# Two plain up tiles ahead of the block sums, and convolution taps in alternation, in a hybrid encoder step

## The chip, the cores and the metric

The kernel runs on one core of a Trainium2 chip. The metric is the device time of one execution in microseconds (us). TensorE multiplies matrices, VectorE (DVE), ScalarE (ACT) and GpSimd (POOL) do elementwise work, SyncE (SP) issues the transfers.

## The reference

One step of an encoder layer for 1024 prompt and 64 sample frames (1088 in all) of width 1024, everything in float32. Four mixers, then attention over a memory of 256 tokens, then a feed-forward part:

```
p = rmsnorm(x) @ w_in                       # split over conv, forgetting attention, HGRN2, stick-breaking
x = x + concat(conv, fox, hgrn, sb) @ w_out
x = x + mem_attend(rmsnorm(x), mk, mv)      # ... @ w_mo at its end
x = x + square(relu(rmsnorm(x) @ w_up)) @ w_down      # 1024 -> 4096 -> 1024
y = rmsnorm(x)
```

The convolution mixer is depthwise over 256 channels with 31 taps: each output frame is the sum of 31 inputs times a weight per channel, plus a bias; a layer norm and silu follow.

## The kernel before

Activations stand with the channels on the 128 partitions and the frames along the row. The frames are cut into group 0 (512 frames) and group 1 (576). Float32 products are made from rounded halves: `split` writes a high part (a cast on ScalarE, L74) and a low part (a subtraction on VectorE, L171), and each block product is three matmuls: high times high, high times low, low times high.

The program is written in Tile: a planner at build time orders each engine's instructions. Among those that are ready it takes the one with the smallest priority number; the number grows with every instruction written, and `tc.cur_priority += n` puts what follows n steps behind. Buffers are slots of a pool per tag ("ap" 16, "xt" 16, "aq" 12, "tm" 4 slots of 576 columns); an instruction waits until its slot is free. Weight tiles have two raw slots (`wr`) and two slots each for the halves (`wh`, `wl`).

**The mixers** (to about 670 us) run as four interleaved lanes: projections, attention, convolution (`lane_conv`) and HGRN2. A lane yields an estimated duration and the lane that is behind goes on; `yield Need(slot)` waits for a projection. The convolution has three blocks of frames (352, 352, 414 columns) and two channel halves (`ct`). Each half is an accumulation in one tile `y`: one instruction for the first tap (L770), 30 for the others (L773), each reading the `y` that the one before wrote. The two halves are written one after the other, and the layer norm (L788 on) needs both.

**The seam.** `dense_add(1, w_mo, ..., after=forms)` (L1297) adds the second half of the memory output product to group 1 for eight weight tiles m in the order 0, 4, 1, 5, 2, 6, 3, 7, stores the row (L1101) and calls `forms(m)` 600 priority steps back. For every m this adds the row's square to a running sum (L1049 to L1054); for m of 4 and above it norms rows k and k + 4 of group 1 (L1075) and builds the operand sums of the next product (L1286 to L1295).

**The up products.** The 32 up tiles go in pairs. With two halves of the width and the two frame groups, a pair is a 2 x 2 by 2 x 2 block product, made from seven instead of eight block products (i, the pair, runs from 0 to 15). The operand sums are T1 to T4; B11, B21 are group 0's halves (`h3`) and B22 the lower half of group 1; the weights have sums S1 to S4 (`sums`, `wform`). Two of the seven products need only group 0 (L1341, L1346 or L1357: bank `W`); the others are made by `mul2` in two strips of 288 columns. Pairs 0 and 1 have an order of their own (`i < 2`). Pair 0 also forms the norm factor `q` of group 1 (L1361 to L1364); it is applied to the results (L1321). The hidden rows go to DRAM (L1379).

Of the kernel before, what the change touches and what calls it, by code (L numbers as in the profile page):

```python
# [17 lines left out]
P = 128  # L18
# [9 lines left out]
CW = 31  # L28
# [24 lines left out]
def kernel(ctx: ExitStack, tc: tile.TileContext, *args):  # L53
# [688 lines left out]
    def lane_conv():  # L742
        tails = [None, None]
        for t0, np_ in ((0, 352), (352, 352), (704, 320)):
            last = t0 + np_ == SP
            n, nt = (CE, np_ + SS) if last else (np_, np_)
            ys, exts = [], []
            for ct in range(2):
                yield Need(ct)
                yield Need(2 + ct)  # L750
                ext = ct_(f"ext{ct}", f"ce{ct}", CE + HW)
                if t0 == 0:
                    V.memset(ext[:, :HW], 0.0)
                else:
                    V.tensor_copy(out=ext[:, :HW], in_=tails[ct])
                nc.sync.dma_start(out=ext[:, HW:HW + np_], in_=pj_d[ct][:, t0:t0 + np_])
                if last:
                    V.tensor_copy(out=ext[:, HW + np_:CE - SS + HW], in_=hT[:, ct])
                    nc.sync.dma_start(out=ext[:, CE - SS + HW:], in_=pj_d[ct][:, SP:T])
                gg, sg = ct_("gg", f"cy{ct}"), ct_("sg", "c0")  # L760
                nc.sync.dma_start(out=gg[:, :nt], in_=pj_d[2 + ct][:, t0:t0 + nt])
                sigmoid(sg[:, :nt], gg[:, :nt])
                V.tensor_tensor(out=ext[:, HW:HW + np_], in0=ext[:, HW:HW + np_], in1=sg[:, :np_], op=ALU.mult)
                if last:
                    V.tensor_tensor(out=ext[:, CE - SS + HW:], in0=ext[:, CE - SS + HW:], in1=sg[:, np_:nt], op=ALU.mult)
                else:
                    tails[ct] = hc.tile([P, HW], F32, name=f"tl{ct}", tag=f"tl{ct}", bufs=2)
                    V.tensor_copy(out=tails[ct], in_=ext[:, n:n + HW])
                y = ct_(f"y{ct}", f"cy{ct}")
                V.tensor_scalar(out=y[:, :n], in0=ext[:, 0:n], scalar1=cwT[:, ct, 0:1], scalar2=cvec[:, 0, ct:ct + 1],  # L770
                                op0=ALU.mult, op1=ALU.add)
                for j in range(1, CW):
                    V.scalar_tensor_tensor(out=y[:, :n], in0=ext[:, j:j + n], scalar=cwT[:, ct, j:j + 1], in1=y[:, :n],  # L773
                                           op0=ALU.mult, op1=ALU.add)
                    if j % 3 == 2:
                        yield 0.15 + n / 300.0
                ys.append(y[:, :n])
                exts.append(ext)
            if last:
                for at, dst in ((np_, conv_p), (CE, conv_s)):  # L780
                    ps = ps_cv.tile([P, G], F32, name="pco", tag="cv")
                    for ct in range(2):
                        nc.tensor.transpose(ps[:HW, ct * P:(ct + 1) * P], exts[ct][:, at:at + HW], ident)
                    ot = ct_("cvo", "c0")
                    V.tensor_copy(out=ot[:HW, :G], in_=ps[:HW])
                    nc.sync.dma_start(out=dst[0, 0], in_=ot[:HW, :G])
            rs = ct_("rs", "c0").rearrange("p (j n) -> p j n", j=2)
            sqs = [ct_(f"sq{ct}", f"ce{ct}", CE + HW) for ct in range(2)]  # L788
            for p0, pn in ((0, n // 2), (n // 2, n - n // 2)):
                yp = [y[:, p0:p0 + pn] for y in ys]  # L790
                sq = [s[:, p0:p0 + pn] for s in sqs]
                pm = ps_cv.tile([P, 512], F32, name="pme", tag="cv")
                for ct in range(2):
                    mm(pm[:, :pn], ones, yp[ct], ct == 0, ct == 1)
                for ct in range(2):
                    V.scalar_tensor_tensor(out=yp[ct], in0=pm[:, :pn], scalar=-1.0 / G, in1=yp[ct],
                                           op0=ALU.mult, op1=ALU.add)
                    act(sq[ct], yp[ct], AF.Square)
                pv2 = ps_cv.tile([P, 512], F32, name="pva", tag="cv")
                for ct in range(2):  # L800
                    mm(pv2[:, :pn], ones, sq[ct], ct == 0, ct == 1)
                v, r, t = rs[:, 0], sq[0], rs[:, 1]
                rstd_chain(None, pn, pv2[:, :pn], "xxx", scale=1.0 / G, out=r, tiles=(v, t))
                for ct in range(2):
                    V.tensor_tensor(out=yp[ct], in0=yp[ct], in1=r, op=ALU.mult)
                    V.tensor_scalar(out=yp[ct], in0=yp[ct], scalar1=cvec[:, 1, ct:ct + 1],
                                    scalar2=cvec[:, 2, ct:ct + 1], op0=ALU.mult, op1=ALU.add)
                for ct in range(2):
                    sigmoid(sq[ct], yp[ct])
                    V.tensor_tensor(out=yp[ct], in0=yp[ct], in1=sq[ct], op=ALU.mult)  # L810
                    if not last or p0 == 0:
                        nc.sync.dma_start(out=mix_d[ct][:, t0 + p0:t0 + p0 + pn], in_=yp[ct])
                    else:
                        nc.sync.dma_start(out=mix_d[ct][:, t0 + p0:SP], in_=ys[ct][:, p0:np_])
                        nc.sync.dma_start(out=mix_d[ct][:, SP:T], in_=ys[ct][:, CE - SS:])
                    yield 0.5 + pn / 150.0
# [449 lines left out]
    hb = {B11: h3[:4], B21: h3[4:]}  # L1266
    for f in (T2, T1, B22):
        hb[f] = [[late.pop(0)() for _ in range(2)] for k in range(4)]
    for f in (T3, T4):
        hb[f] = [[unit("xt" if k else "ap", F32R) for _ in range(2)] for k in range(4)]  # L1270

    sums2 = []

    def forms(m):

        if m == 0:
            sums2.append(add_square(1, 0, None, unit("tm")))
        else:
            add_square(1, m, sums2[0], unit("tm"))
        if m < 4:  # L1280
            return
        k = m - 4
        (h11, h12), (h21, h22) = ((xw[0][i], xw[1][i]) for i in (k, k + 4))
        for i in (k, k + 4):
            normed(1, i, g_ffn, rm1, 0, N2, xw[1][i])
        V.tensor_tensor(out=h11[:, :N1], in0=h12[:, :N1], in1=h11[:, :N1], op=ALU.subtract)  # L1286
        act(h11[:, N1:], h12[:, N1:], AF.Copy)
        split(*hb[T1][k], h11)
        V.tensor_tensor(out=h12, in0=h22, in1=h12, op=ALU.subtract)
        split(*hb[B22][k], h22)  # L1290
        V.tensor_tensor(out=h22, in0=h22, in1=h11, op=ALU.subtract)
        split(*hb[T2][k], h22)
        split(*hb[T3][k], h12)
        V.tensor_tensor(out=h21[:, :N1], in0=h21[:, :N1], in1=h22[:, :N1], op=ALU.subtract)
        split(hb[T4][k][0][:, :N1], hb[T4][k][1][:, :N1], h21[:, :N1])  # L1295

    dense_add(1, w_mo, HALF * P, KD - HALF, om[HALF:], ps1, store=True, after=forms)  # L1297
    pm1.close()
    psm = ctx.enter_context(tc.tile_pool(name="psm", bufs=2, space=PSUM))
    tc.cur_priority += 1200  # L1300
    for t in t1s:
        Q.memset(t[:, N1:], 0.0)

# [20 lines left out]
    def plus(out, a, b, eng=V):  # L1324
        eng.tensor_tensor(out=out, in0=a, in1=b, op=ALU.add)  # L1325

    for i in range(NU):
        r1 = fetch_w(w_up, 0, KD, 2 * i * P)
        r2 = fetch_w(w_up, 0, KD, (2 * i + 1) * P)
        pa, pb = ([wp.tile([P, KD, P], F32R, name=nm, tag=nm) for nm in ("wh", "wl")] for _ in range(2))  # L1330
        split(*pa, r1)
        s1 = fz.tile([P, 4, P], F32, name="s1", tag="s1", bufs=1)
        sums(r1[:, :4], r1[:, 4:], r2[:, :4], r2[:, 4:], s1, V)
        S2, S1 = wform(r1[:, :4]), wform(s1)
# [6 lines left out]
        mul(W, [t[:, :4] for t in pa], hb[B11], True, slice(0, N1))  # L1341
        act(t1[:, :N1], W, AF.Copy)
        c12, c22 = unit("ap"), unit("ap")
        if i < 2:

            mul(W, [t[:, 4:] for t in pa], hb[B21], False, slice(0, N1))  # L1346
            Y = banks()
            mul2(Y, S4, hb[B22], True)
            plus(halves(c12), halves(t1), Y[:, :, :HN])
        mul2(Z, S2, hb[T2], True)  # L1350
        plus(halves(c12), halves(c12 if i < 2 else t1), Z[:, :, :HN])
        mul2(X, S1, hb[T1], True)
        plus(halves(c22), halves(t1), X[:, :, :HN])
        if i < 2:
            plus(halves(c12), halves(c12), X[:, :, :HN])
        else:
            mul(W, [t[:, 4:] for t in pa], hb[B21], False, slice(0, N1))  # L1357
        c11 = unit("xt")
        square(c11[:, :N1], W)
        if i == 0:  # L1360
            q = rms_stats(1, psm, "w", s2=sums2[0])  # L1361
            rms = unit("tm")
            nc.sync.dma_start(out=rms, in_=rms_d)
            V.tensor_tensor(out=q, in0=q, in1=rms, op=ALU.mult)  # L1364
        mul2(Z, S3, hb[T3], False)
        plus(halves(c22), halves(c22), Z[:, :, :HN])
        square(c22, c22, q)
        if i >= 2:
            mul2(X, S4, hb[B22], False)
            plus(halves(c12), halves(c12), X[:, :, :HN])  # L1370
        square(c12, c12, q)
# [2 lines left out]
        plus(c21[:, :HN], t1[:, :HN], Z[:, 0, :HN])  # L1374
        plus(c21[:, HN:N1], t1[:, HN:N1], Z[:, 1, :N1 - HN])
        square(c21[:, :N1], c21[:, :N1])
        for m, g, t in ((0, 0, c11), (0, 1, c12), (1, 0, c21), (1, 1, c22)):
            t0, n, _ = GR[g]
            nc.sync.dma_start(out=hid_d[2 * i + m][:, t0:t0 + n], in_=t[:, :n])  # L1379
    fz_ctx.close()  # L1380


# [122 lines left out]
```

## Time and profile before

| | |
|---|---|
| median of 3 runs | 1795.35 us (1791.69 to 1795.78) |
| profiled execution, its own time | 1796.39 us |
| its span, first to last instruction | 1794.7 us |
| TensorE matmuls busy | 1721.9 us (96%) |
| VectorE busy | 1179.9 us (66%) |
| ScalarE busy | 793.2 us (44%) |
| GpSimd busy | 103.2 us (6%) |
| mean granted TensorE clock | 0.987 |

The span lies within the profiled execution's time; 1.7 us are outside it. Matmuls overlap in the pipeline, so their durations add up to more than their spacing; what one costs is read from the distance of their starts.

### The profile page before, as it was taken

What the parts mean: (1) busy time and instruction counts of PE and PEld (TensorE: products, weight loads), DVE (VectorE), ACT (ScalarE), POOL (GpSimd) and SP (SyncE); (2) the same over time, 40 slices, a digit from 0 to 9 for tenths busy, and PEclk for the clock granted to TensorE, in tenths of its full rate; (3) what the DMA queues carried; (4) which work ended last, traced back from release to release, by engine and by line L of the source; (5) the groups of instructions that cost most, each with busy time, mean ns of one, the idle gap of its engine ahead of it and who ended that gap; (6) DMA issues with size and microseconds to landing.
All of it is one profiled execution on the core that took longest, in us unless ns stands there. A gap on an engine that the chain in (4) does not pass through costs nothing.

```text
span 1794.7 us, 29493 instructions
## 1 busy us (share of the span) xinstructions
PE 1721.9 (96%) x11463; PEld 1511.7 (84%) x11475; DVE 1179.9 (66%) x2242; ACT 793.2 (44%) x1615; POOL 103.2 (6%) x201
## 2 busy tenths in 40 slices
PE   7999999999999999999999959999999999999997
PEld 5877757887877788988899949999999999999987
DVE  6455779888979886667777796555556544444435
ACT  6464566456356764346456343433344221222213
POOL 3011202000320210000000000000000000000000
PEclk9999999999999999999999989999999999999999
DMA  8221212222232448232522413333234823332112
GB/s 251 78 78 37 65 47 76 70 68 80 64 116 89 141 139 279 87 95 65 159 77 72 123 49 106 104 116 106 98 97 168 294 90 97 98 97 67 42 35 100
DMA packets 227307, 184.86 MB, mean 103 GB/s; under 512 B 16478, under 2 KB 196127, under 8 KB 227167
## 3 DMA queue, kind: packets, MB, share of 16 engines
q1 hardware_dynamic: 226911, 182.96, 32.7%
q8 instruction: 90, 1.47, 0.3%
q14 instruction: 50, 0.41, 0.1%
q0 software_dynamic: 256, 0.01, 0.0%
HBM read 132.45 MB, written 50.44 MB: 102 GB/s over the span
## 4 chain that ended last, share of the span: by engine, by line
PE 57%; DVE 5%; DMA 2%; ACT 1%; issue 1%; POOL 0%; SPq 0%; DVEq 0%; ACTq 0%; POOLq 0%
PE pz L71 23%; PE pw L71 16%; PE pa L71 8%; PE pq L71 5%; PE pmo L71 1%; PE pms L71 1%; DMA kr<-mkT_d 1%; PE pm L71 1%; DVE wl L171 1%; DVE ap L171 0%; PE pmt L1160 0%; PE pz L1430 0%; DVE tm L1075 0%; ACT wh L74 0%; DMA mix_d<-ho 0%
## 5 line engine op out<-in xcount | busy, mean ns | idle before, releaser
L74 ACT ACTIVATE wh<-wr 128x1024 fp32r<-128x1024 f32 (+1 forms) x180 | 161.4, 905 | 436.5 <-PE pz L71 196.3
L171 DVE TENSOR_TENSOR wl<-wr,wh 128x1024 fp32r<-128x1024 f32 (+1 forms) x180 | 184.6, 1032 | 70.8 <-ACT wh L74 69.8
L71 PE MATMUL pw<-ap,wh 128*128 128x512 f32 x704 | 219.7, 393 | 1.3 <-ACT t L74 0.7
L71 PE MATMUL pz<-ap,wh 128*128 128x288 f32 x960 | 192.5, 294 | 0.4 <-DVE ap L1325 0.4
L71 PE MATMUL pa<-ap,wh 128*128 128x256 f32 (+2 forms) x768 | 187.6, 332 | 2.6 <-DVE xt L1099 2.2
L71 PE MATMUL pm<-hx,wh 128*128 128x512 f32 (+1 forms) x640 | 176.3, 363 | 1.1 <-DVE hx L283 0.8
L71 PE MATMUL pm<-ap,wh 128*128 128x256 f32 (+1 forms) x768 | 164.2, 307 | 0.6 <-ACT vn L74 0.6
L71 PEld LDWEIGHTS pz<-ap,wh 128*128 128x128 f32 x960 | 156.7, 188 | 5.3 <-DVE ap L1325 0.8
L71 PEld LDWEIGHTS pw<-ap,wh 128*128 128x128 f32 x704 | 127.8, 189 | 23.7 <-ACT t L74 1.1
L71 PEld LDWEIGHTS pa<-ap,wh 128*128 128x128 f32 x768 | 132.9, 192 | 13.5 <-DVE xt L1099 2.4
L71 PE MATMUL pw<-ap,wl 128*128 128x512 f32 x352 | 138.1, 392 | 5.6 <-DVE wl L171 5.6
L71 PE MATMUL pz<-ap,wl 128*128 128x288 f32 x480 | 141.0, 294 | 0.0
L71 PEld LDWEIGHTS pm<-ap,wh 128*128 128x128 f32 x768 | 123.5, 191 | 5.4 <-issue 2.1
L71 PE MATMUL pa<-ap,wl 128*128 128x512 f32 (+2 forms) x384 | 127.2, 332 | 0.0
L71 PEld LDWEIGHTS pm<-hx,wh 128*128 128x128 f32 x640 | 110.2, 191 | 19.7 <-issue 1.9
L1325 DVE TENSOR_TENSOR xt<-xt,pz 128x576 f32<-128x576 f32 x56 | 42.2, 753 | 115.5 <-PE pz L71 111.0
L71 PE MATMUL pm<-ap,wl 128*128 128x256 f32 (+1 forms) x384 | 114.1, 297 | 0.0
L71 PE MATMUL pm<-hx,wl 128*128 128x512 f32 (+1 forms) x320 | 112.3, 351 | 0.0
L773 DVE SCALAR_TENSOR_TENSOR y<-ext,cwT,y 128x352 f32<-128x352 f32 (+1 forms) x180 | 106.4, 607 | 1.6
L1325 DVE TENSOR_TENSOR xt<-xt,pw 128x512 f32<-128x512 f32 (+2 forms) x80 | 51.0, 638 | 69.8 <-PE pw L71 67.7
L71 PE MATMUL pq<-ap,wh 128*128 128x512 f32 (+2 forms) x384 | 93.0, 331 | 0.0
L74 ACT ACTIVATE sba<-sba 128x127 f32<-128x127 f32 (+8 forms) x102 | 68.1, 682 | 52.8 <-DVE sba L490 52.0
(376 smaller groups left out, 3645.1 us busy)
## 6 DMA issues: line engine op xcount, KB each, us to landing
wr<-in_w_up_dram SPq DMA_DIRECT2D x32, 512.0 KB
wr<-in_w_down_dram SPq DMA_DIRECT2D x32, 512.0 KB
wr<-in_w_in_dram SPq DMA_DIRECT2D x24, 512.0 KB
hid_d<-ap SPq DMA_DIRECT2D x32, 288.0 KB
aq<-hid_d SPq DMA_DIRECT2D x32, 288.0 KB
wr<-in_w_out_dram SPq DMA_DIRECT2D x16, 512.0 KB
wr<-in_w_mq_dram SPq DMA_DIRECT2D x16, 512.0 KB
wr<-in_w_mo_dram SPq DMA_DIRECT2D x32, 256.0 KB
```

The source lines that it names most:

```text
L71: nc.tensor.matmul(out, lhsT=lhsT, rhs=rhs, start=start, stop=stop, **kw)
L74: nc.scalar.activation(out=out, in_=in_, func=func, **kw)
L171: V.tensor_tensor(out=lo, in0=src, in1=hi.bitcast(F32), op=ALU.subtract)
L773: V.scalar_tensor_tensor(out=y[:, :n], in0=ext[:, j:j + n], scalar=cwT[:, ct, j:j + 1], in1=y[:, :n], op0=ALU.mult, op1=ALU.add)
L1325: eng.tensor_tensor(out=out, in0=a, in1=b, op=ALU.add)
```

## The change

Pair 0 is no longer made from block sums. Its two tiles are plain products over the whole width: for group 0 with `h3`, for group 1 with the normed rows themselves. For that, all eight rows of group 1 are normed and split (four into the new pairs `b12`, four into B22 as before), in `second(m)` right after each row is complete. The operand sums (`forms`, now without norm and B22) are written in pair 1, after its first weight split, and 800 priority steps back; the step of 1200 ahead of the pairs is gone. Pair 1 keeps the order that pairs 0 and 1 had. In the convolution the taps of the two channel halves alternate, so both halves' projections have to be there before the first tap. The slots for T3 and T4 are taken after the output product.

```diff
                     V.tensor_copy(out=tails[ct], in_=ext[:, n:n + HW])
-                y = ct_(f"y{ct}", f"cy{ct}")
-                V.tensor_scalar(out=y[:, :n], in0=ext[:, 0:n], ...)
-                for j in range(1, CW):
-                    V.scalar_tensor_tensor(out=y[:, :n], in0=ext[:, j:j + n], scalar=cwT[:, ct, j:j + 1], in1=y[:, :n],
-                                           op0=ALU.mult, op1=ALU.add)
-                    if j % 3 == 2:
-                        yield 0.15 + n / 300.0
-                ys.append(y[:, :n])
+                ys.append(ct_(f"y{ct}", f"cy{ct}")[:, :n])
                 exts.append(ext)
+            for j in range(CW):
+                for ct, (y, ext) in enumerate(zip(ys, exts)):
+                    if j == 0:
+                        V.tensor_scalar(out=y, in0=ext[:, 0:n], ...)
+                    else:
+                        V.scalar_tensor_tensor(out=y, in0=ext[:, j:j + n], scalar=cwT[:, ct, j:j + 1], in1=y,
+                                               op0=ALU.mult, op1=ALU.add)
+                if j % 3 == 2:
+                    yield 0.3 + n / 150.0
...
-    for f in (T3, T4):
-        hb[f] = [[unit("xt" if k else "ap", F32R) for _ in range(2)] for k in range(4)]
+    b12 = [pair(1) for k in range(4)]
     sums2 = []
-    def forms(m):
+    def second(m):
         if m == 0:
             sums2.append(add_square(1, 0, None, unit("tm")))
         else:
             add_square(1, m, sums2[0], unit("tm"))
-        if m < 4:
-            return
-        k = m - 4
+        normed(1, m, g_ffn, rm1, 0, N2, xw[1][m])
+        split(*(hb[B22][m - 4] if m >= 4 else b12[m]), xw[1][m])
+    def forms(k):
         (h11, h12), (h21, h22) = ((xw[0][i], xw[1][i]) for i in (k, k + 4))
-        for i in (k, k + 4):
-            normed(1, i, g_ffn, rm1, 0, N2, xw[1][i])
...
-        split(*hb[B22][k], h22)
...
-    dense_add(1, w_mo, HALF * P, KD - HALF, om[HALF:], ps1, store=True, after=forms)
+    dense_add(1, w_mo, HALF * P, KD - HALF, om[HALF:], ps1, store=True, after=second)
     pm1.close()
     psm = ctx.enter_context(tc.tile_pool(name="psm", bufs=2, space=PSUM))
-    tc.cur_priority += 1200
+    for f in (T3, T4):
+        hb[f] = [[unit("xt" if k else "ap", F32R) for _ in range(2)] for k in range(4)]
...
-    for i in range(NU):
+    def store_hidden(i, tiles):
+        for m, g, t in zip((0, 0, 1, 1), (0, 1, 0, 1), tiles):
+            t0, n, _ = GR[g]
+            nc.sync.dma_start(out=hid_d[2 * i + m][:, t0:t0 + n], in_=t[:, :n])
+    ws = [load_w(w_up, 0, KD, m * P) for m in range(2)]
+    tiles = [unit("ap") for _ in range(4)]
+    for m in range(2):
+        W = bank()
+        mul(W, ws[m], hb[B11] + hb[B21], True, slice(0, N1))
+        square(tiles[2 * m][:, :N1], W)
+    q, rms = rms_stats(1, psm, "w", s2=sums2[0]), unit("tm")
+    nc.sync.dma_start(out=rms, in_=rms_d)
+    V.tensor_tensor(out=q, in0=q, in1=rms, op=ALU.mult)
+    for m in range(2):
+        Z = banks()
+        mul2(Z, ws[m], b12 + hb[B22], True)
+        square(halves(tiles[2 * m + 1]), Z[:, :, :HN], halves(q))
+    store_hidden(0, tiles)
+    for i in range(1, NU):
         r1 = fetch_w(w_up, 0, KD, 2 * i * P)
         r2 = fetch_w(w_up, 0, KD, (2 * i + 1) * P)
         pa, pb = ([wp.tile([P, KD, P], F32R, name=nm, tag=nm) for nm in ("wh", "wl")] for _ in range(2))
         split(*pa, r1)
+        if i == 1:
+            tc.cur_priority += 800
+            for k in range(4):
+                forms(k)
```

Further down `i < 2` becomes `i == 1`, the statistic of pair 0 (L1360 to L1364) leaves the loop, and the loop's stores go through `store_hidden`.

## Rows read from the trace of the kernel before

**Rows 1.** The page's strip: TensorE's busy tenths in 40 slices of 44.9 us.

```profile
PE   7999999999999999999999959999999999999997
```

**Rows 2.** Windows over the seam: busy us of each engine, granted clock, share and rate of DMA.

```profile
1040.00:1050.00 10.00, 1.44 (x2) 0.50 (x2) 10.00 (x16) 4.44 (x8) 0.00 (x0) 0.50 0.00 0
...
1033.40:1080.00 46.60, 27.65 (x156) 23.29 (x157) 43.65 (x69) 20.93 (x37) 0.00 (x0) 0.82 0.17 51
```

**Rows 3.** TensorE's waits, 1033 to 1080 us: in total, times, longest.

```profile
PE pr L71 <- DVE tm L1054: 10.7, 1, 10.7
PE pw L71 <- DVE wl L171: 5.6, 1, 5.6
...
PE pw L71 <- ACT t L74: 0.7, 1, 0.7
```

**Rows 4.** TensorE's timeline in the seam: start, us, what, idle before and releaser.

```profile
1033.92 0.70 PE L71 MATMUL pw<-ap,wh 128*128 128x512 f32 x2 [0.61 <-ACT wh L74]
1045.29 1.44 PE L71 MATMUL pr<-tm,ones 128*128 128x320 f32 x2 [10.67 <-DVE tm L1054]
...
1052.96 1.05 PE L71 MATMUL pw<-ap,wh 128*128 128x512 f32 x2
...
1055.52 0.71 PE L71 MATMUL pw<-ap,wh 128*128 128x512 f32 x2
...
1058.64 0.61 PE L71 MATMUL pw<-ap,wh 128*128 128x512 f32 x2
...
1059.32 0.61 PE L71 MATMUL pw<-ap,wh 128*128 128x512 f32 x2
...
1060.91 0.70 PE L71 MATMUL pr<-tm,ones 128*128 128x256 f32 x2 [0.75 <-ACT xt L74]
1061.94 0.53 PE L71 MATMUL pz<-fz,wh 128*128 128x288 f32 x2 [0.34 <-ACT wh L74]
...
1063.36 0.42 PE L71 MATMUL pz<-fz,wh 128*128 128x288 f32 x2
...
1064.94 0.43 PE L71 MATMUL pz<-fz,wh 128*128 128x288 f32 x2
```

**Rows 5.** VectorE's timeline: first and last of its run, two spacings.

```profile
1013.67 0.82 DVE L1075 SCALAR_TENSOR_TENSOR xt<-xt,g_ffn,tm 128x576 f32<-128x576 f32 x1 [0.46 <-DMA x_d<-xt]
...
1035.20 0.75 DVE L171 TENSOR_TENSOR fz<-xt,fz 128x576 fp32r<-128x576 f32 x1
1035.87 0.75 DVE L171 TENSOR_TENSOR xt<-xt 128x576 fp32r<-128x576 f32 x1
...
1051.09 1.22 DVE L171 TENSOR_TENSOR wl<-wr,wh 128x1024 fp32r<-128x1024 f32 x1
1052.22 0.75 DVE L171 TENSOR_TENSOR fz<-xt,fz 128x576 fp32r<-128x576 f32 x1
...
1062.66 0.68 DVE L171 TENSOR_TENSOR ap<-wr,ap 128x512 fp32r<-128x512 f32 x1
```

**Rows 6.** The statistic's operations on tile tm: min/median/max ns.

```profile
L152 DVE TENSOR_TENSOR tm<-tm x2: 424/458/493, 1063.8 to 1065.6; 128x320 f32<-128x320 f32 x1, 128x256 f32<-128x256 f32 x1
```

**Rows 7.** The chain that ended last, one transfer of it: start, us.

```profile
1063.37 4.59 DMA wr<-in_w_up_dram
```

**Rows 8.** SP's timeline behind the seam.

```profile
1076.30 2.86 SPq L1379 DMA_DIRECT2D hid_d<-ap  x2
```

**Rows 9.** VectorE's timeline in the mixers: runs of taps.

```profile
323.97 4.92 DVE L773 SCALAR_TENSOR_TENSOR y<-ext,cwT,y 128x352 f32<-128x352 f32 x8
...
454.81 2.56 DVE L773 SCALAR_TENSOR_TENSOR y<-ext,cwT,y 128x352 f32<-128x352 f32 x5
```

**Rows 10.** Windows: L773 alone (VectorE, clock, DMA); then all engines.

```profile
300.00:345.00 45.00, 14.29 (x25) 0.92 0.22 67
...
520.00:540.00 20.00, 16.41 (x138) 13.75 (x138) 17.64 (x38) 10.22 (x29) 10.16 (x12) 1.00 0.27 86
```

**Rows 11.** SP's timeline: the loads of group 1's mixer outputs.

```profile
677.16 5.16 SPq L1016 DMA_DIRECT2D aq<-mix_d  x8
```

More of the change, by code (lines that the diff above doesn't have):

```diff
@@ L768, in lane_conv @@
                     V.tensor_copy(out=tails[ct], in_=ext[:, n:n + HW])
-                y = ct_(f"y{ct}", f"cy{ct}")
-                V.tensor_scalar(out=y[:, :n], in0=ext[:, 0:n], scalar1=cwT[:, ct, 0:1], scalar2=cvec[:, 0, ct:ct + 1],
-                                op0=ALU.mult, op1=ALU.add)
-                for j in range(1, CW):
-                    V.scalar_tensor_tensor(out=y[:, :n], in0=ext[:, j:j + n], scalar=cwT[:, ct, j:j + 1], in1=y[:, :n],
-                                           op0=ALU.mult, op1=ALU.add)
-                    if j % 3 == 2:
-                        yield 0.15 + n / 300.0
-                ys.append(y[:, :n])
-                exts.append(ext)
+                ys.append(ct_(f"y{ct}", f"cy{ct}")[:, :n])
+                exts.append(ext)
+            for j in range(CW):
+                for ct, (y, ext) in enumerate(zip(ys, exts)):
+                    if j == 0:
+                        V.tensor_scalar(out=y, in0=ext[:, 0:n], scalar1=cwT[:, ct, 0:1], scalar2=cvec[:, 0, ct:ct + 1],
+                                        op0=ALU.mult, op1=ALU.add)
+                    else:
+                        V.scalar_tensor_tensor(out=y, in0=ext[:, j:j + n], scalar=cwT[:, ct, j:j + 1], in1=y,
+                                               op0=ALU.mult, op1=ALU.add)
+                if j % 3 == 2:
+                    yield 0.3 + n / 150.0
             if last:
@@ L1343 @@
         c12, c22 = unit("ap"), unit("ap")
-        if i < 2:
+        if i == 1:
             mul(W, [t[:, 4:] for t in pa], hb[B21], False, slice(0, N1))
@@ L1350 @@
         mul2(Z, S2, hb[T2], True)
-        plus(halves(c12), halves(c12 if i < 2 else t1), Z[:, :, :HN])
+        plus(halves(c12), halves(c12 if i == 1 else t1), Z[:, :, :HN])
         mul2(X, S1, hb[T1], True)
         plus(halves(c22), halves(t1), X[:, :, :HN])
-        if i < 2:
+        if i == 1:
             plus(halves(c12), halves(c12), X[:, :, :HN])
@@ L1359 @@
         square(c11[:, :N1], W)
[L1360 to L1364, printed above, removed]
         mul2(Z, S3, hb[T3], False)
@@ L1367 @@
         square(c22, c22, q)
-        if i >= 2:
+        if i > 1:
             mul2(X, S4, hb[B22], False)
@@ L1376 @@
         square(c21[:, :N1], c21[:, :N1])
-        for m, g, t in ((0, 0, c11), (0, 1, c12), (1, 0, c21), (1, 1, c22)):
-            t0, n, _ = GR[g]
-            nc.sync.dma_start(out=hid_d[2 * i + m][:, t0:t0 + n], in_=t[:, :n])
+        store_hidden(i, (c11, c12, c21, c22))
     fz_ctx.close()
```

## The prediction, made before the change was run

> **What bounds the kernel now.** I read the page's strip of slices first. TensorE is at 9 tenths nearly everywhere; the one deep hole after the start is slice 24, about 1032 to 1077 us [rows 1]. A table by windows sizes it: from 1033.4 to 1080 TensorE is busy 27.65 of 46.60 us, so 18.95 us are idle, and from 1040 to 1050 the granted clock is 0.50, the 1.2 GHz level [rows 2]. That is the seam between the second memory output product (dense_add, L1297) and the first pair of up tiles. The waits name the cause: 10.7 us for a sum of squares (L1054) and 5.6 us for a weight split (L171), both on VectorE, and 0.7 us for a ScalarE copy [rows 3]. The timeline of VectorE shows why: its queue runs without a hole worth naming from 1013.67 to about 1063.3, through the operand sums (`forms`) that all seven products of the first pair need [rows 5]. So in this seam VectorE's queue is the bound; before and behind it, TensorE.
>
> The timeline of TensorE also gives the prices [rows 4]. At full clock three 512-column matmuls take 1059.32 − 1058.64 = 0.68 us, 0.227 each; twelve of 288 columns take 1064.94 − 1063.36 = 1.58, 0.132 each (those of 224 I price by columns, 0.102). At the lower level six of 512 take 1055.52 − 1052.96 = 2.56, 0.427 each. About ten ran so: 10 × 0.20 = 2.0 us. The statistic's first product lost another 0.6 (1.44 us, against 0.70 × 320/256 = 0.88 at the later one's rate). The seam thus loses 18.95 + 2.0 + 0.6 = 21.55 us. That is the pool from which the change can draw.
>
> **The change, part by part.**
>
> *TensorE's own work.* A pair by block sums is 24 products of 512 columns (5.44 us), 96 of 288 (12.64), and 12 each of 288 and 224 (2.81): 20.89 us. The plain pair is 48 of 512 (10.88) and 96 of 288 (12.64): 23.52 us. The change adds 2.63 us for good; only i = 0 is exchanged, and i = 1 keeps the early form that both i < 2 had.
>
> *What the hole becomes.* The plain pair's 48 wide products need only group 0 (`h3`, ready long before) and the two weight splits. The first weights' splits no longer stand 1200 behind the sums in priority: their VectorE half, at 1051.09 before [rows 5], should fall near 1032. So TensorE goes on at about 1033.9, after the same 0.6 us wait as now [rows 4]. The wide products last to 1044.8, the statistic's (0.70 + 0.88) to 1046.4, the 96 narrow ones to 1059.0. These need all eight group 1 splits. Per weight tile VectorE has two adds of 576 columns together, a weight split of 512, and then sum, norm and split of 576: with an operation of 576 every 0.67 [rows 5] and the others by columns 0.67 + 0.60 + 3 × 0.67 = 3.3 us, against 24 matmuls of 288 columns in the mean, 3.2 us. It falls only a few microseconds behind and ends near 1041 if the later sums stay behind it, so the narrow products find their operands.
>
> Then i = 1: its two group 0 products take 2.72 each, with the 0.7 us copy wait between them, to 1065.1. From there everything needs `forms`, the weight sums and their splits. VectorE's run gains, over before: four splits of `b12` (4 × 0.67 = 2.68); two weight splits more (1052.22 − 1051.09 = 1.13 each, 2.26); the rest of the statistic, seven narrow operations that lay behind the run (about 0.46 long, some 0.08 of it overlapped [rows 5, 6]: 2.6); the product with the stored factor (0.67); two squares of the plain pair (1.34). That is 9.55 us, so the run ends at 1063.3 + 9.55 = 1072.8. Now the first narrow product starts at 1061.94, 1.3 before the run's end [rows 4]; by the same lead it would start at 1071.5. TensorE stands still for 1071.5 − 1065.1 = 6.4 us. Behind a wait of 5.6 us, after one of 10.7, the clock was at its lower level [rows 2, 3]; I charge the same 2.0 us.
>
> New loss: 2.63 + 6.4 + 2.0 + 0.6 + 0.7 = 12.33 us. Gain in the seam: 21.55 − 12.33 = **9.2 us**. Bounds: the wait and its clock are nothing if the planner puts enough sums early (gain 17.6); some 5 us more if the narrow plain products also wait, because sums slip ahead of the group 1 splits (gain about 4).
>
> *Transfers.* The weights of i = 1 need 4.59 us to land [rows 7]. Their buffers come free at the two early splits, not at the end of a pair, so they land near 1040: hidden under the plain pair. On SP they stand in the program behind the plain pair's four stores. Today the planner lets fetches pass: pair 1's leave at 1063.37 [rows 7], two of pair 0's stores at 1076.30 [rows 8]. Without that cover the fetch would wait for the last store, near 1061, and land near 1070. The weights of i = 2 start near 1073 and have the 15.5 us of i = 1's last products over them, as before. ScalarE gains four `b12` casts and the plain tiles' squares; it is not the late one in any wait above 0.7 us here. GpSimd has only two memsets.
>
> *The convolution.* The number of taps stays 186. Taps that follow each other at once came every (4.92 − 0.57)/7 = 0.62 us at 324 us and every (2.56 − 0.57)/4 = 0.50 at 455 [rows 9], 0.57 being one tap's length. I read the first as one half waiting for its own last tap, and the second as both halves mixed by the planner. Alternation then saves 0.12 us for each pair that stands together: nothing if other work always lies between, at most 174 × 0.12 = 21 us of VectorE. But TensorE bounds this stage, with at most 3.6 us idle in 20 (520 to 540 [rows 10]). Against it, 25 taps that now run in 300 to 345 [rows 10] wait for the second half's projections; their 14.29 us move later. This costs nothing while the convolution's end is hidden: its last outputs are loaded at 677.16 to 682.3 [rows 11], in the second of eight weight tiles of group 0's output product, and group 1 starts six tiles later (6 × 24 × 0.227 = 32.7 us). I take a gain of 1 us; bounds, a gain or a loss of 4, the deepest idle stretch.
>
> The Trainium skill speaks against this part: "VectorE: DVE Perf Modes", section "The DRAIN you can't avoid", says that each operation drains before the next starts and that leaving out waits between them saves nothing. By it this term is 0 and the sum is 1 us higher. The two spacings of one and the same shape [rows 9] do not fit that, so I keep the row.
>
> **Sum.** 1796.39 − 9.2 − 1 = 1786.2 us against the profiled run; the median lies 1.04 lower, so **1785 us**, 0.6% faster.
>
> **Rivals.**
> - *VectorE keeps up.* The planner fills gaps with the weight sums early, as it did between the last forms. Wait and clock loss vanish: 17.6 in the seam, up to 4 in the mixers: 1773 to 1780. For it: the 9.55 us rest on pitches without any idle time won. Against: the run of before had hardly any idle time to fill.
> - *A longer wait in the second half of the seam.* The narrow plain products, or the fetch behind the stores on SP, come late: gain 4 to 6 us, 1787 to 1791.
> - *It does not do what it says.* The early weight split still lands behind the sums, as at 1051.09 now; the wide products start there, the hole stays, and the pair costs 2.63 more: gain within 5 us, 1790 to 1798. Against: the 1200 steps of priority go.
> - *Slower: the convolution ends too late.* Where its last output slips by more than 32.7 − 5.2 = 27.5 us, group 1's output product waits, one for one. To undo the seam it must slip by about 37 us, 2.6 times the 14.29 us that are moved; with 45 us of slip the time is 1804. The slack makes this unlikely.
>
> **How the numbers follow.** Forecast as worked out (gain 7 to 14): 0.50. VectorE keeps up: 0.18. The longer wait: 0.14, most of it still a little above 5.4 us. No effect: 0.12. The late convolution: 0.06. About 0.3% (5.4 us) is what a measurement can tell from no change: faster 0.79, same 0.15, slower 0.06. The range runs from the middle of the first rival, 1775, to the end of the second, 1791. The likeliest alone is 1781 to 1788.
>
> **What the profile would show.** Right: the 10.7 us wait for L1054 is gone; wide matmuls run on from 1034 at clock 1.00; a wait of some 6 us for VectorE or ScalarE lies near 1065, before i = 1's first narrow product; the stretch of i = 1 ends about 9 us earlier. Wrong: no such wait (first rival), waits before the narrow plain products or for a weight transfer (second), a weight split near 1050 (third), output products that wait for the convolution's last load (fourth). The tap spacing settles the convolution: 0.50 for 352 columns throughout, or 0.62 still.

## The result, and the profile after

The changed kernel takes 1786.58 us (median of 9 runs, 1781.03 to 1789.9); the kernel before, on the same chip, 1795.35 us (9 runs). The ratio is 0.9947, 95% interval 0.9928 to 0.9965: 0.5% faster. The forecast was 1785, with a range of 1775 to 1791. The profiled execution after took 1784.25 us, its span is 1782.5.

The strip of the page shows first that the deep hole of [rows 1] is gone. Slice 24, now 1025 to 1069 us, went from 5 to 8 tenths:

```profile
PE   7999999999998999999999989999999999999997
```

Windows over the seam of the changed kernel (columns as in [rows 2]):

```profile
1031.00:1060.00 29.00, 28.28 (x165) 25.03 (x163) 28.88 (x48) 17.90 (x31) 0.00 (x0) 1.00 0.28 88
1060.00:1080.00 20.00, 13.48 (x72) 12.30 (x73) 15.48 (x24) 7.55 (x12) 0.00 (x0) 0.83 0.26 78
```

Up to 1060 TensorE is busy at a granted clock of 1.00; before, 1040 to 1050 had 1.44 us of work in 10 at 0.50 [rows 2]. The remaining hole lies in 1060 to 1080. TensorE's waits from 1030 to 1080 us, beside [rows 3]:

```profile
PE pz L71 <- ACT wh L74: 5.9, 1, 5.9
PE pw L71 <- ACT t L74: 0.7, 1, 0.7
PE pw L71 <- DVE xt L1102: 0.6, 1, 0.6
```

The waits of 10.7 and 5.6 us went; one of 5.9 came. TensorE's timeline puts it in its place, beside [rows 4]:

```profile
1032.17 0.69 PE L71 MATMUL pw<-ap,wh 128*128 128x512 f32 x2 [0.64 <-DVE xt L1102]
...
1057.02 0.62 PE L71 MATMUL pw<-ap,wh 128*128 128x512 f32 x2
...
1060.61 0.73 PE L71 MATMUL pw<-ap,wh 128*128 128x512 f32 x2 [0.69 <-ACT t L74]
...
1069.48 0.85 PE L71 MATMUL pz<-fz,wh 128*128 128x288 f32 x2 [5.86 <-ACT wh L74]
...
1071.03 0.68 PE L71 MATMUL pz<-fz,wh 128*128 128x288 f32 x2
...
1073.91 0.68 PE L71 MATMUL pz<-fz,wh 128*128 128x288 f32 x2
...
1074.58 0.43 PE L71 MATMUL pz<-fz,wh 128*128 128x288 f32 x2
...
1111.62 4.13 PE L71 MATMUL pz<-aq,ap 128*128 128x288 f32 x30
```

The plain pair starts at 1032.17, pair 1's group 0 products at 1057.02, and then TensorE stands still for 5.86 us ahead of pair 1's first narrow product. Behind it twelve matmuls of 288 columns take 1073.91 − 1071.03 = 2.88 us, 0.24 each; at full clock they take 0.132 [rows 4]. The releaser is a cast on ScalarE, but VectorE's timeline, beside [rows 5], tells who is late:

```profile
1029.40 1.23 DVE L171 TENSOR_TENSOR wl<-wr,wh 128x1024 fp32r<-128x1024 f32 x1
...
1068.07 0.69 DVE L1316 TENSOR_TENSOR wr<-wr 128x512 f32<-128x512 f32 x1
...
1070.47 0.70 DVE L171 TENSOR_TENSOR ap<-wr,ap 128x512 fp32r<-128x512 f32 x1
1075.65 0.75 DVE L1327 TENSOR_TENSOR ap<-t,pz 128x576 f32<-128x576 f32 x1 [4.48 <-PE pz L71]
```

The first weight split, at 1051.09 before, is now at 1029.40. The last weight sum (L1316) ends at 1068.76; ScalarE casts it at 1068.79 for 0.63 us, and TensorE starts at 1069.48. VectorE's queue has no hole worth naming until its end at 1071.17, as before. ScalarE, in its timeline just ahead of that cast, itself stands waiting for VectorE:

```profile
1067.59 0.63 ACT L74 ACTIVATE ap<-wr 128x512 fp32r<-128x512 f32 x1 [0.64 <-DVE wr L1315]
1068.13 0.61 ACT L74 ACTIVATE ap<-s 128x512 fp32r<-128x512 f32 x1
1068.79 0.63 ACT L74 ACTIVATE wh<-wr 128x512 fp32r<-128x512 f32 x1
```

**A yardstick for the seam.** Profiles of single executions differ ahead of the seam as well: in the eleven kernels below the first wide product of pair 0 starts anywhere from 1029.68 to 1038.78 us, 9.1 us apart, nearly the whole effect. So I measure the seam from the first wide product to the run of 30 narrow matmuls in pair 3 (the last line of TensorE's timeline above). Its counterpart in the kernel before:

```profile
1123.57 4.13 PE L71 MATMUL pz<-aq,ap 128*128 128x288 f32 x30
```

With the 1033.92 of [rows 4] this makes 89.65 us before, and 1111.62 − 1032.17 = 79.45 after: **10.20 us** won. The 12.2 us between the two spans are these 10.20, 1.75 us that the first wide product starts earlier, and 0.25 us behind pair 3 (671.13 against 670.88 us to the end; all eleven kernels take 670.6 to 671.1 us there).

### The profile page after: what moved, and what is told of

Its sections match the earlier page's. It is cut to its first block, busy times and chain, and to the rows that moved or that the text cites. A ratio compares the mean times of both kernels' runs of the same rounds, so it can differ in the third digit from the quotient of the medians.

```text
span 1782.5 us, 29501 instructions
## 1 busy us (share of the span) xinstructions
PE 1724.1 (97%) x11475; PEld 1514.2 (85%) x11475; DVE 1174.1 (66%) x2231; ACT 792.0 (44%) x1614; POOL 98.7 (6%) x201
## 4 chain that ended last, share of the span: by engine, by line
PE 57%; DVE 3%; ACT 1%; issue 0%; DMA 0%; DVEq 0%; ACTq 0%
PE pz L71 23%; PE pw L71 16%; PE pa L71 9%; PE pq L71 5%; PE pmo L71 1%; PE pms L71 1%; DVE ap L171 1%; DVE wl L171 0%; PE pmt L1163 0%; PE pz L1450 0%; DMA kr<-mkT_d 0%; DVE tm L1078 0%; DVE xt L171 0%; DVE aq L171 0%; PE pr L71 0%
## 5 line engine op out<-in xcount | busy, mean ns | idle before, releaser
L71 PE MATMUL pw<-ap,wh 128*128 128x512 f32 x720 | 223.4, 391 | 1.3 <-ACT t L74 0.7
L71 PE MATMUL pz<-ap,wh 128*128 128x288 f32 x988 | 198.3, 294 | 0.0
L71 PEld LDWEIGHTS pz<-ap,wh 128*128 128x128 f32 x988 | 161.3, 188 | 4.7
L71 PE MATMUL pz<-ap,wl 128*128 128x288 f32 x494 | 145.4, 294 | 0.0
L778 DVE SCALAR_TENSOR_TENSOR y<-ext,cwT,y 128x352 f32<-128x352 f32 (+1 forms) x180 | 102.4, 600 | 1.0
L71 PEld LDWEIGHTS pz<-ap,wl 128*128 128x128 f32 x494 | 92.7, 188 | 0.0
```

The lines of the kernel that those rows point to most:

```text
L71: nc.tensor.matmul(out, lhsT=lhsT, rhs=rhs, start=start, stop=stop, **kw)
L778: V.scalar_tensor_tensor(out=y, in0=ext[:, j:j + n], scalar=cwT[:, ct, j:j + 1], in1=y, op0=ALU.mult, op1=ALU.add)
```

## The experiments

All are compared with the kernel before, run on the same chip each time; "seam" is the stretch just defined, from one profile. (The expectations of e1 to e3 give as the seam another stretch, from the end of the memory output product to i = 2's first product.)

| kernel | median, us (runs) | ratio, 95% interval | seam, us |
|---|---|---|---|
| changed kernel | 1786.58 (9) | 0.9947 (0.9928 to 0.9965) | 79.45 |
| e1 seam alone | 1785.56 (6) | 0.9949 (0.9928 to 0.9969) | 79.68 |
| e2 convolution alone | 1794.61 (11) | 0.9998 (0.9985 to 1.001) | 89.37 |
| e3 sums for T3, T4 later | 1778.67 (6) | 0.9905 (0.9888 to 0.9923) | 70.66 |
| e4 two plain pairs | 1775.53 (4) | 0.9894 (0.988 to 0.9908) | 72.52 |
| e5 22 spare matmuls | 1784.92 (5) | 0.9939 (0.9927 to 0.9951) | 78.84 |
| e6 step of 1200 kept | 1789.09 (4) | 0.9958 (0.9944 to 0.9972) | 81.67 |
| e7 more for VectorE | 1788.14 (5) | 0.9961 (0.9946 to 0.9975) | 82.35 |
| e8 before, sums later | 1792.08 (12) | 0.9977 (0.9965 to 0.999) | 86.07 |
| e9 29 spare matmuls | 1784.09 (4) | 0.9938 (0.9917 to 0.9959) | 78.18 |

By the medians e3 and e4 are clear of the changed kernel, e2 and e8 lie on the other side (e8's interval begins where the changed kernel's ends). The intervals of e1, e5, e6, e7 and e9 overlap with the changed kernel's: what is said of these five against it rests on the seam of one profile each. Where the code of the seam is the same, the seam repeats within 0.3 us: e1 and the changed kernel 79.68 and 79.45, e2 and the kernel before 89.37 and 89.65.

My theory: the seam gives the gain, VectorE's queue bounds what is left there, and the low clock is the price of standing still; the convolution gives nothing. Rivals: the convolution gives a part; ScalarE or a transfer sets the wait; the clock falls for a reason of its own.

**e1 and e2: one part alone.** e1 is the changed kernel with the taps as before; e2 the kernel before with this edit alone:

```diff
-                for j in range(1, CW):
-                    V.scalar_tensor_tensor(out=y[:, :n], in0=ext[:, j:j + n], ...)
+            for j in range(CW):
+                for ct, (y, ext) in enumerate(zip(ys, exts)):
+                    ...
```

> Seam alone: the convolution runs as before, one channel half after the other. Theory (the gain lies in the seam, bound by VectorE's queue): the time of the changed kernel, 1786 us within 2, ratio to before about 0.995; from the end of the memory output product to i = 2's first product still about 57 us; taps back at about 106 us of VectorE, which costs nothing while TensorE bounds that stage. Rival (the convolution gives part of the gain): 1 to 4 us slower than the changed kernel, lost ahead of 740 us.

> Convolution alone: the taps alternate, the seam is as before. Theory: the kernel before within 0.2%, although the taps take about 4 us less of VectorE; the seam is 67.5 us again. Rival: 1 to 4 us faster than before (the four microseconds of VectorE come back on the span). Second rival: slower, because the last outputs are loaded later.

Both came out by the theory, within what the times can tell. e1 has the changed kernel's time and seam. e2 has the time of the kernel before; its interval leaves room for a gain of 2.7 us or a loss of 1.8 at most, so that the smaller half of the rival's 1 to 4 us is not ruled out. VectorE does get time back. The windows from 300 to 642 us, the taps' line alone (busy us, clock, DMA), in the kernel before:

```profile
300.00:642.00 342.00, 105.87 (x180) 0.99 0.30 88
```

and in e2:

```profile
300.00:642.00 342.00, 101.86 (x180) 0.99 0.30 89
```

Some 4 us of VectorE are saved, in a stage that TensorE bounds; in the medians of e2 they don't show. In e2's own profile the first wide product starts at 1029.68, 4.24 us earlier than before, which looks like those 4 us. The medians do not bear it out: a kernel's median less its seam is 1706.1 us in the mean of the eight kernels with the new taps, and 1705.9 in that of the three with the old. And e8, with the old taps, starts as late as 1038.78: this part of a single profile scatters.

**e3: fewer operations ahead of the late product.** T3 and T4 are read by pair 1's last two products only. Their part of `forms` becomes `rest`, behind pair 1's weight sums:

```diff
+    def rest(k):
         split(*hb[T3][k], h12)
         V.tensor_tensor(out=h21[:, :N1], in0=h21[:, :N1], in1=h22[:, :N1], op=ALU.subtract)
         split(hb[T4][k][0][:, :N1], hb[T4][k][1][:, :N1], h21[:, :N1])
...
         split(*S4, r1[:, 4:])
+        if i == 1:
+            for k in range(4):
+                rest(k)
```

> The changed kernel, with the operand sums and splits that only i = 1's last two products read (T3, T4) issued behind i = 1's weight sums and splits: some 7.5 us of VectorE leave the queue ahead of i = 1's first narrow product. Theory (the wait of 5.9 us is VectorE's queue, and the low clock behind it comes with the wait): wait and low clock go, about 8 us faster than the changed kernel, near 1778, seam 49 to 50 us. Rival (ScalarE's cast or a transfer sets the wait): the wait stays at 5 to 6 us, time as the changed kernel. Second rival: the wait goes to i = 1's last products, no gain.

The wait and the low clock are gone, TensorE is busy from 1060 to 1080 throughout, and the seam is 8.79 us shorter. This version beats both kernels. Windows of e3, columns as in [rows 2]:

```profile
1060.00:1080.00 20.00, 20.00 (x142) 19.27 (x142) 19.76 (x33) 10.44 (x18) 0.00 (x0) 1.00 0.29 96
```

and its timeline:

```profile
1030.07 0.70 PE L71 MATMUL pw<-ap,wh 128*128 128x512 f32 x2 [0.63 <-DVE xt L1102]
...
1061.17 0.42 PE L71 MATMUL pz<-fz,wh 128*128 128x288 f32 x2
...
1068.33 0.95 PE L71 MATMUL pz<-fz,ap 128*128 128x288 f32 x6
...
1100.73 4.13 PE L71 MATMUL pz<-aq,ap 128*128 128x288 f32 x30
```

The first narrow product of pair 1 comes 31.10 us after the first wide one, against 37.31 in the changed kernel: 6.21 us are the wait and the restart behind it. From there to the next group of six (1079.22 in the changed kernel) it takes 7.16 us against 9.74: 2.58 us are the clock. No transfer that pair 1 needs was relieved by the edit: its weights are asked for 1.5 us before and 1.7 us behind the first wide product in both kernels. ScalarE was, of the casts that belong to T3 and T4; but it had been waiting for VectorE, as its timeline above shows, and e7 below loads VectorE alone.

**e4: two plain pairs.** Pairs 0 and 1 plain, block sums from pair 2 on (`for i in range(2)` around the plain pair, `for i in range(2, NU)` behind it).

> Two plain pairs, i = 0 and i = 1, block sums from i = 2. Theory: the second plain pair costs TensorE 2.63 us more, the operand sums have 23.5 us more of cover, so the 5.9 us wait and about 2.4 us of low clock go: 5 to 6 us faster than the changed kernel, near 1781. Rival (the wait belongs to the first pair by block sums wherever it stands): the wait moves with it, 2.6 us slower than the changed kernel.

The only wait of TensorE left from 1026 to 1140 us is the 0.6 at the start:

```profile
PE pw L71 <- DVE xt L1102: 0.6, 1, 0.6
```

So the rival, a wait that moves along, falls. The seam is 6.93 us shorter than in the changed kernel and 1.86 longer than e3's. e3 still has the copy wait of 0.7 us, so a plain pair costs about 1.86 + 0.69 = 2.55 us, beside the 2.63 that were worked out. By the medians e4 is the faster of the two, by the seam e3; their intervals overlap, so which is better is open. Both lie wholly below the changed kernel's interval. The median of e4 is 11 us below the changed kernel's, where 5 to 6 were expected; 6.93 of them are the seam, and the rest is not explained.

**e5 and e9: the wait filled with work.** Matmuls of 512 columns into a bank that nobody reads, 22 in e5 and 29 in e9:

```diff
             mul(W, [t[:, 4:] for t in pa], hb[B21], False, slice(0, N1))
+            idle = bank()
+            for _ in range(22):
+                mm(idle, pa[0][:, 4], hb[B21][0][0][:, :N1], True, True)
```

> The changed kernel with 22 spare matmuls of 512 columns put between i = 1's group 0 products and its first narrow product, into a bank that nobody reads (22 x 0.227 = 5.0 us, inside the wait of 5.9). Theory (the low clock behind the wait is the price of standing still): the first narrow product starts when it did, and the twelve matmuls behind it run at 0.132 instead of 0.24 each: about 2.4 us faster than the changed kernel. Rival (the clock falls there for another reason, or the spare matmuls only delay): no gain, or up to 2 us slower.

> As e5, with 29 spare matmuls (29 x 0.227 = 6.6 us), so that the whole stretch between i = 1's group 0 products and its first narrow product is covered; with 22 of them 1.75 us of standing still were left and the clock fell all the same. Theory (any standing still of this size costs the low clock, no matter how it is shortened): no wait, granted clock 1.00 from 1060 to 1080, the narrow matmuls at 0.132 from the first on, the stretch from the first wide product to i = 3 about 2.5 us shorter than in the changed kernel (77 us against 79.45). Rival (the clock falls there for another reason, such as the kind of matmul that starts): the slow matmuls stay, stretch 78.8 us or more.

e5 did not answer as expected: the first narrow product starts where it did (37.28 us after the first wide one), but the seam is only 0.61 us shorter. TensorE's timeline of e5 shows that 1.75 us of standing still were left, and that the matmuls ran at half speed all the same:

```profile
1072.66 0.53 PE L71 MATMUL pz<-fz,wh 128*128 128x288 f32 x2 [1.75 <-ACT wh L74]
...
1074.07 0.68 PE L71 MATMUL pz<-fz,wh 128*128 128x288 f32 x2
...
1076.95 0.64 PE L71 MATMUL pz<-fz,wh 128*128 128x288 f32 x2
...
1081.80 0.95 PE L71 MATMUL pz<-fz,ap 128*128 128x288 f32 x6
```

Twelve matmuls from 1074.07 to 1076.95, 2.88 us, are 0.24 each, as behind the wait of 5.86. Still, the stretch from the first narrow product to the group of six takes 1081.80 − 1072.66 = 9.14 us against 9.74. e5 could not tell the two theories apart, and e9 covers the rest. There a wait of 0.2 us is left and the clock stays up (windows of e9):

```profile
1060.00:1080.00 20.00, 19.71 (x123) 17.82 (x122) 15.78 (x25) 8.18 (x13) 0.00 (x0) 1.00 0.23 66
```

In its timeline the same stretch, first narrow product to the group of six, takes 1075.36 − 1067.76 = 7.60 us against 9.74:

```profile
1067.76 0.54 PE L71 MATMUL pz<-fz,wh 128*128 128x288 f32 x2 [0.21 <-ACT wh L74]
...
1075.36 0.95 PE L71 MATMUL pz<-fz,ap 128*128 128x288 f32 x6
...
1082.82 0.54 PE L71 MATMUL pz<-ap,wh 128*128 128x288 f32 x2 [0.57 <-DVE ap L1327]
```

The low clock alone thus cost 2.14 us. Of these 0.84 are lost again later (the way from the group of six to pair 2's run of 30 is 12.10 us, against 11.26), most of it in a new wait of 0.57 us for VectorE, so that the seam is 1.27 us shorter and not 2.5. The direction and the clock are the theory's; the rival would have kept the slow matmuls. The medians (1784.09 and 1786.58) are too close to show a gain of this size.

**e6: the step kept.** `tc.cur_priority += 1200` stands again ahead of the plain pair's weight loads.

> The changed kernel with the step of 1200 in priority put back ahead of the plain pair's weight loads, as it stood before. Theory (VectorE's queue is one run whose length counts): the plain pair's weight splits fall behind the group 1 squares, norms and splits, a wait of 8 to 10 us opens ahead of the first wide product, the wait of 5.9 us at i = 1 vanishes because the sums still end near 1071: net 3 to 4 us slower than the changed kernel. Rival (each wait stands by itself): 8 to 10 us slower.

The seam is 2.22 us longer, a little less than expected, and my way there was wrong. The weight splits slipped only to 1035.47 and 1038.01, among the group 1 work and not behind it. TensorE's waits of e6 from 1022 to 1110 us:

```profile
PE pz L71 <- ACT wh L74: 3.7, 1, 3.7
PE pw L71 <- DVE wl L171: 1.8, 1, 1.8
PE pw L71 <- DVE xt L1102: 1.0, 1, 1.0
```

What opened early (1.8 and 0.3 us) came off the later wait (5.86 to 3.66): one queue of fixed length, not two waits that add. So the waits are as long together as before, and the 2.2 us are the clock once more: the slow stretch at pair 1 stays (10.46 us from the first narrow product to the group of six, against 9.74), and a second one opens behind the wait of 1.8 us, where wide products run at a mean granted clock of 0.72 (window of e6):

```profile
1037.00:1043.00 6.00, 6.00 (x20) 4.74 (x20) 6.00 (x9) 1.37 (x2) 0.00 (x0) 0.72 0.61 175
```

That is some 0.28 × 6 = 1.7 us there, and 0.7 at pair 1.

**e7: more work for VectorE.** Eight subtractions of 512 columns more:

```diff
     def forms(k):
         (h11, h12), (h21, h22) = ...
+        for _ in range(2):
+            V.tensor_tensor(out=t1s[0][:, :N1], in0=h12[:, :N1], in1=h11[:, :N1], op=ALU.subtract)
```

> The changed kernel with eight more subtractions of 512 columns on VectorE, two in front of each of the four operand sums, written to a tile that is overwritten later. Theory (VectorE's run ends last): 8 x 0.6 = 4.8 us; the wait of 5.9 us grows by 4.8 to 5.3 and the time by as much, 1791. Rival (a transfer or ScalarE sets the wait): no change.

The seam is 2.90 us longer, not 4.8. VectorE's run does end 4.8 us later: its last split ends 43.82 us after the first wide product (1034.85 in e7), against 39.00. But the planner put the weight sums ahead of the last operand sums, so the first narrow product starts when it did (36.97 us after the first wide one, against 37.31). The timelines of VectorE (its last split) and TensorE (the first narrow product) in e7:

```profile
1077.98 0.69 DVE L171 TENSOR_TENSOR wl<-wr,wh 128x512 fp32r<-128x512 f32 x1
...
1071.82 0.85 PE L71 MATMUL pz<-fz,wh 128*128 128x288 f32 x2 [5.54 <-DVE xt L1293]
```

The wait comes in two pieces, with a few matmuls between them:

```profile
PE pz L71 <- DVE xt L1293: 5.5, 1, 5.5
PE pz L71 <- ACT ap L74: 2.5, 1, 2.5
```

The two waits make 8.1 us, against 5.86: work for VectorE alone lengthens them, though the order of its run counts as well as its length. The rival, no change, falls in the seam; the medians (1788.14 and 1786.58) are too close to show it.

**e8: the late sums without a plain pair.** The kernel before with `rest` behind pair 0's weight sums.

> The kernel before, without a plain pair, but with the operand sums and splits for T3 and T4 issued behind i = 0's weight sums and splits. Theory: 7.5 us leave VectorE's queue ahead of i = 0's weight splits, the two holes shrink by 6 to 7.5 us in all, near 1788; what the plain pair then still brings is the rest, about 9 us against e3. Rival (the order alone is the whole gain of e3): 1778 to 1780. Second rival: the holes move to i = 0's last products, no gain.

The seam is 3.58 us shorter, half of what I expected. TensorE's waits of e8 from 1022 to 1110 us, beside [rows 3]:

```profile
PE pr L71 <- DVE tm L1054: 6.6, 1, 6.6
PE pw L71 <- DVE wl L171: 5.1, 1, 5.1
PE pz L71 <- ACT wh L74: 2.4, 1, 2.4
```

The 10.7 fell to 6.6, the 5.6 hardly moved, and a new wait of 2.4 us came ahead of pair 1's first narrow product: without the plain pair TensorE stood still there. With it the same edit is worth 8.79 us. The order of the sums alone does not explain e3; the plain pair gives the cover, the order uses it. One rival was not tried: the kernel before with the late sums and without the step of 1200, whose weight splits would come early too. How much of the gain needs the plain pair, and how much only early weight splits, stays open.

## Why the prediction was right

- **The bound and the place of the gain** held: 10.20 us in the seam, where 9.2 were worked out, and nothing measurable elsewhere (e1, e2). The term is 1.0 us too small. By the medians the gain is 8.8 us, which the scatter of the runs can't tell from 10.2 or from 9.2.
- **VectorE's run** was to grow by 9.55 us. From the first wide product to its end it went from 1063.34 − 1033.92 = 29.42 [rows 4, 5] to 1071.17 − 1032.17 = 39.00 us: 9.58. The run starts 20.3 us ahead of the first wide product in both kernels, and it has 96 operations where it had 80: the sixteen that were counted.
- **The new wait** was to be 6.4 us, and is 5.86. The first narrow product has a lead of 1.69 us over the run's end, and not 1.3: in both kernels four splits stand behind the last weight sum, but before, one operation of the statistic stood there too, and ScalarE began the cast that TensorE needs 0.74 us behind the sum, and now 0.03. In the kernel before, the sum (VectorE) and the cast (ScalarE) were these:

```profile
1059.85 0.68 DVE L1314 TENSOR_TENSOR wr<-wr 128x512 f32<-128x512 f32 x1
...
1061.27 0.62 ACT L74 ACTIVATE wh<-wr 128x512 fp32r<-128x512 f32 x1
```

  e3, e6 and e7 show that VectorE's queue sets the wait. The profile names ScalarE there, whose cast of 0.63 us only passes on a late sum.
- **The clock behind it**, taken as 2.0, costs 2.14 by e9 and 2.58 by e3.
- **The dearer pair**, 2.63, is 2.55 by e4 against e3. The two small waits, 0.6 and 0.7, stayed. The measured terms make 2.55 + 5.86 + 2.14 to 2.58 + 0.64 + 0.69 = 11.9 to 12.3 us of new loss (12.33 in the prediction). Set against the old 21.55 this is a gain of 9.2 to 9.7; the 10.20 hold 0.5 to 1.0 more. It is the old hole that was taken too small: e4, with two plain pairs and no wait in the seam, takes 72.52 us, so by estimate a seam without plain pairs and without waits would take 72.52 − 2 × 2.55 = 67.42. The kernel before thus loses 22.23 there and the changed one 12.03; the prediction, less the 0.6 that lie ahead of the first wide product, had 20.95 and 11.73. Which part of the old hole was missed, the runs do not show.
- **Transfers** are hidden, as forecast: pair 1's weights are asked for at 1030.65 and 1033.92, right after the early splits, and no wait of TensorE names a transfer. ScalarE does wait 4.9 us for pair 2's weights, until 1074.87, with no wait of TensorE behind it.
- **The convolution** is the term that failed, in a step and probably in its size. No gain shows where I took 1 us (e2: from a gain of 2.7 to a loss of 1.8, so 1 us is not excluded). And the 25 taps in 300 to 345 us, which were to wait for the second half's projections, did not move: they take 13.69 us there now (14.29 before, [rows 10]). That both halves' projections have to be there before the first tap, as the section on the change says, is not so: the planner still runs one half's taps while the other half waits. VectorE's timeline of the changed kernel shows both kinds, and the first tap (L775) of the second half behind the one run and ahead of the other:

```profile
324.37 4.93 DVE L778 SCALAR_TENSOR_TENSOR y<-ext,cwT,y 128x352 f32<-128x352 f32 x8
...
343.13 0.46 DVE L775 TENSOR_SCALAR y<-ext,cwT,cvec 128x352 f32<-128x352 f32 x1
...
424.23 0.45 DVE L775 TENSOR_SCALAR y<-ext,cwT,cvec 128x352 f32<-128x352 f32 x1
...
426.23 4.05 DVE L778 SCALAR_TENSOR_TENSOR y<-ext,cwT,y 128x352 f32<-128x352 f32 x8
```

  The first run is one half alone, (4.93 − 0.57)/7 = 0.62 us apart; in the second both halves are open, and the taps are 0.50 apart. This bears out the reading of [rows 9]. By the section of the Trainium skill that was weighed there ("VectorE: DVE Perf Modes", "The DRAIN you can't avoid") there was no gain to be had. The time of e2 does not contradict it; the two spacings do not fit its sentence on waits that save nothing, though the section adds that a next operation that is not held starts earlier. What VectorE saves in a stage that TensorE bounds did not show in the time, which is the argument that the prediction gave and then put at 1 us.
- **The rivals.** "VectorE keeps up" did not come by itself, but e3, one edit away, lands within its 1773 to 1780: 1778.67 us. The waits of the second rival, the late split and the late convolution did not occur.

## What to carry to other kernels

Where an engine's queue is the bound of a seam, count its operations up to the one that the next engine waits for: work moved ahead of it costs, and the cheapest gain here was to send behind it what is read later (T3 and T4, 8.8 us, with the plain pair as cover). Giving the waiting engine dearer work that needs nothing late pays as long as its surcharge (2.55 us) is less than the wait and the clock that it covers. Compare seams between two marks inside the trace, not by spans: ahead of this seam single executions differed by up to 9 us.

## What the runs showed of the hardware

A wait of 1.75 us (e5) cost most of what one of 5.86 cost in half-speed work: from the first narrow product to the group of six it takes 9.14 us behind the one, 9.74 behind the other, and 7.60 without a wait of note (e9). In the changed kernel the granted clock fell during the wait; in e5 it fell after TensorE had already begun again, with the first matmuls still at full speed. Windows of the changed kernel (the first line) and of e5, columns as in [rows 2]:

```profile
1067.40:1069.40 2.00, 0.00 (x0) 0.00 (x0) 2.00 (x5) 1.75 (x4) 0.00 (x0) 0.57 0.34 131
...
1070.60:1072.60 2.00, 0.31 (x2) 0.00 (x0) 2.00 (x5) 1.77 (x4) 0.00 (x0) 1.00 0.34 131
1072.60:1074.60 2.00, 1.84 (x10) 1.61 (x11) 1.75 (x3) 0.53 (x2) 0.00 (x0) 0.85 0.00 0
```

The waits of 0.6 and 0.7 us were not followed by a lower clock (1.00 from 1031 to 1060 us in the changed kernel, and from 1060 to 1080 in e3). Filling most of the wait gave back 0.6 us of the clock's loss; filling it whole, 2.14.

On VectorE, multiply-and-add operations on 352 float32 columns started 0.62 us apart where each reads the result of the one before, and 0.50 apart where two independent sums were open.
